# An encoder on one core: input and memory also laid out feature-major by the host, and the residual's chunks issued behind the second block of weights

## The chip, the cores and the metric

One core of one Trainium2 chip runs the whole kernel in one launch. The metric is the device time of an execution in microseconds; the time before is 2916.61 us, the median of three runs (2915.35 to 2917.63). The engines are named as the profile names them: PE (TensorE, the matrix engine) with its weight loads PEld, DVE (VectorE), ACT (ScalarE), POOL (GpSimd) and SP (SyncE), which issues most of the transfers.

## What is computed

Two layers of an encoder trunk over 256 tokens of 2048 features, in float32, with 256 memory tokens. Cut to what matters here:

```python
for layer in range(2):
    h = rms_norm(x, norm_mix_g[layer])
    if layer == 0:                       # conv module and differential attention, one input projection
        z = h @ ab_w_in                  # 2048 -> val 1024, gate 1024, q 1024, k 1024, v 1024
        a_out = silu(layer_norm(depthwise_conv(val * sigmoid(gate))))
        b_out = diff_attention(q, k, v)  # 8 heads, needs lambda from four small vectors
        x = x + concat(a_out, b_out) @ ab_w_out
    else:
        x = x + mixer_s5(h, ...)         # diagonal state space, forward and backward
    xn, memn = rms_norm(x, norm_xa_g[layer]), rms_norm(mem, norm_mem_g[layer])
    x = x + cross_attention(xn, memn)    # 4 heads; k = memn @ xa_wk, v = memn @ xa_wv
    x = x + conv_ffn(rms_norm(x, norm_ffn_g[layer]))
return rms_norm(x, final_g)
```

`rms_norm(x, g)` is `x * rsqrt(mean(x*x) + eps) * g`, the mean over the features of a token.

## The kernel before

**Products.** Every float32 operand of a large product is split in two: an upper part `hi` (rounded to the matrix engine's float32r type) and a lower part `lo` (the rest), and a product is the sum of hi x hi, hi x lo and lo x hi. The weights come from memory in tiles ("blocks") of 128 x 1024 elements, 512 KB. `wtile` (L204) issues the transfer of one on SP (L208; the very first one on ACT's queue), rounds it to `hi` on ACT (L214) and subtracts on DVE to get `lo` (L216). Four `raw` buffers and three each of `hi` and `lo` let this run ahead of PE. `lin_ws` (L242) multiplies with the weights as the stationary operand: 16 steps of 128 features, each with two products of 512 columns (`hi` against both parts of x, L254) and two of 256 columns (`lo` against x's upper part, L255), four steps to a tile of weights. `lin_xs` (L266, products in L289) does it with x as the stationary operand.

**The feature-major operand.** A product sums over features, so x must stand with features on the partitions. `transpose_chunk` (L150) makes this from 512 features of a token-major chunk: 8 transposes on PE through `ident` into two PSUM tiles `ps_xt` (L160), and from these four upper parts on ACT, scaled by the norm's gain (L167), and four lower parts on DVE (L168); the result is one buffer `x2` of four steps. The factor rstd of the norm is applied after the product: `sumsq` (L128) takes sums of squares on ACT (L132), `norm_end` (L183) turns them into `rstd` by a chain of small operations on DVE (L112 to L122, L137 and L138) and spreads it over the partitions with four small products on PE, `rb` (L147).

**The start.** `setup` (L79) loads `ident`, the first chunk of X and the gains. `mixer0` (L351) then multiplies x with the blocks of `ab_w_in`: four pairs of val and gate. For the first val block `xt_first` (L194) brings X's other three chunks in on SP (L199), one step ahead of their use, and transposes each. Behind the first `lin_ws` stand five loads of small constants (L376), the squares of X, and `norm_end`; `rb2` is used first by the first gate. `lambda` of the differential attention comes after the gates (L397 to L401).

**The memory.** `mem_T` (L305) is called after the projections of the first layer (`mem_T(0)`) and behind the first feed-forward network for the second layer (`mem_T(1)`). For layer 0 it loads all of the memory token-major into `mm`, in slot A1 (L312), sums its squares and makes the four chunks with `transpose_chunk`; for layer 1 it loads it again in eight pieces of 256 KB, `mst` (two buffers, L320), and transposes with other gains. `mem_kv` (L333) multiplies with `xa_wv` and `xa_wk`.

**Side work.** While weights stream, pieces of other work go to DVE, ACT and POOL: parameters of the state space, the convolution. `background` (L220) plays them behind each tile of weights by credits (`RATE`, L32). In the same manner `self.loads` holds loads that wait for a tile of weights: `wtile` takes one entry from it behind each tile's transfer (`load_one`, L554), until now for the heads of the cross-attention only. The framework's scheduler then sets the order on each engine, so that instructions may come earlier or later than the code has them.

## Time and profile before

| what | value |
|---|---|
| median of three runs (lowest to highest) | 2916.61 us (2915.35 to 2917.63) |
| the profiled execution: its own time | 2915.32 us |
| the profiled execution: span of the trace | 2913.5 us |
| PE busy | 2869.7 us, 98% |
| DVE busy | 2203.7 us, 76% |
| ACT busy | 1492.0 us, 51% |
| POOL busy | 266.0 us, 9% |
| DMA | 674.16 MB, mean 231 GB/s |

The busy shares are means over the whole span, in which the stages differ; the span is that of the profiled execution, 1.8 us shorter than the execution's own time, and that lies 1.3 us below the median. PE's row is the one nearest to the span. Matmuls overlap in a pipeline, so the length of one in the trace is not what it costs: what one costs is read from how far it pushes the next start.

### The profile page before, as it was taken

The numbers are of one execution on the slowest core, as the hardware profiler recorded it, in microseconds if no ns is written. First come the engines' busy times: TensorE is split into PE (matmuls) and PEld (weight loads), VectorE is DVE, ScalarE is ACT, GpSimd is POOL, SyncE is SP. The second block draws the span as 40 slices with busy tenths as digits, with TensorE's granted clock in tenths as the row PEclk, the third lists the DMA queues.
The fourth block names the chain that finished last, engine by engine and source line by source line (L and its number), as shares of the span: only waits on it lengthen the run. The fifth ranks groups of instructions, "written<-read, shape, count | busy, mean of one in ns | idle before, by whom it ended". The sixth has DMA issues, their size and how long they took to land. (4 is left out here: it accounts for less than half of the span.)

```text
span 2913.5 us, 44430 instructions
## 1 busy us (share of the span) xinstructions
PE 2869.7 (98%) x16769; PEld 2426.1 (83%) x16769; DVE 2203.7 (76%) x3524; ACT 1492.0 (51%) x2015; POOL 266.0 (9%) x504
## 2 busy tenths in 40 slices
PE   8999999999999999999999999999999999999998
PEld 7887887788888888888887787788888888888887
DVE  8899987877899987889855895556557776467765
ACT  6545654444555543455544554545445555345543
POOL 2000022222220012020021121000000000000000
PEclk9999999999999999999999999999999999999999
DMA  7655569978897688777797887665455555655554
GB/s 233 227 192 171 191 216 306 295 238 286 295 313 242 229 276 254 267 252 240 235 316 271 291 331 275 208 197 185 159 200 184 193 185 191 194 188 191 186 194 159
DMA packets 206503, 674.16 MB, mean 231 GB/s; under 512 B 33392, under 2 KB 36208, under 8 KB 205776
## 3 DMA queue, kind: packets, MB, share of 16 engines
q1 hardware_dynamic: 177952, 593.97, 61.5%
q0 software_dynamic: 28192, 76.83, 8.0%
q8 instruction: 131, 2.15, 0.3%
q14 instruction: 84, 0.69, 0.1%
q10 hardware_dynamic: 144, 0.52, 0.0%
HBM read 620.48 MB, written 61.08 MB: 234 GB/s over the span
## 5 line engine op out<-in xcount | busy, mean ns | idle before, releaser
L216 DVE TENSOR_TENSOR lo<-raw,hi 128x1024 fp32r<-128x1024 f32 x960 | 1173.1, 1223 | 539.9 <-ACT hi L214 535.8
L214 ACT CAST hi<-raw 128x1024 fp32r<-128x1024 f32 x960 | 1008.8, 1052 | 983.1 <-PE ps_xs L289 430.7
L254 PE MATMUL ps_ws<-x,hi 128*128 128x512 f32 x4352 | 1351.4, 396 | 2.8 <-DVE x L168 1.2
L255 PEld LDWEIGHTS ps_ws<-x,lo 128*128 128x128 f32 x4352 | 793.6, 188 | 186.6 <-DVE lo L216 10.5
L255 PE MATMUL ps_ws<-x,lo 128*128 128x256 f32 x4352 | 844.7, 280 | 6.7 <-DVE lo L216 6.6
L254 PEld LDWEIGHTS ps_ws<-x,hi 128*128 128x128 f32 x4352 | 674.5, 189 | 17.3 <-ACT hi L214 2.5
L289 PE MATMUL ps_xs<-hi,hb 128*128 128x512 f32 x1328 | 357.6, 390 | 0.0
L289 PEld LDWEIGHTS ps_xs<-hi,hb 128*128 128x128 f32 x1328 | 248.9, 188 | 51.7
L289 PE MATMUL ps_xs<-lo,hb 128*128 128x512 f32 x664 | 204.9, 390 | 0.0
L289 PE MATMUL ps_xs<-hi,x 128*128 128x512 f32 x640 | 177.5, 394 | 1.5 <-ACT hi L214 1.5
L852 POOL DMA_DIRECT2D w1s<-d_pw x256 | 122.8, 488 | 602.5 <-DVE w1s L845 318.2
L289 PEld LDWEIGHTS ps_xs<-hi,x 128*128 128x128 f32 x640 | 119.1, 188 | 32.0 <-issue 6.2
L289 PEld LDWEIGHTS ps_xs<-lo,hb 128*128 128x128 f32 x664 | 124.3, 188 | 25.5
L289 PE MATMUL ps_xs<-hi,oT 128*128 128x512 f32 x512 | 141.1, 392 | 0.8 <-ACT hi L214 0.8
L289 PE MATMUL ps_xs<-hi,gT 128*128 128x512 f32 x512 | 138.2, 391 | 0.3 <-ACT hi L214 0.3
L262 ACT COPY z<-ps_ws 128x512 f32<-128x512 f32 x88 | 51.7, 587 | 145.2 <-PE ps_ws L254 145.2
L289 PEld LDWEIGHTS ps_xs<-hi,gT 128*128 128x128 f32 x512 | 95.7, 188 | 21.2 <-issue 0.8
L289 PEld LDWEIGHTS ps_xs<-hi,oT 128*128 128x128 f32 x512 | 95.3, 188 | 20.1 <-ACT hi L214 1.0
L656 ACT ACTIVATE c<-z,fdb,fdw 128x256 f32<-128x256 f32 x176 | 96.3, 595 | 30.5 <-DVE z L651 30.4
L511 DVE SCALAR_TENSOR_TENSOR av<-hpt,cdw,av 128x256 f32<-128x256 f32 x240 | 109.8, 484 | 0.5
L263 DVE TENSOR_TENSOR z<-ps_ws,z 128x512 f32<-128x512 f32 x88 | 60.7, 690 | 56.0 <-ACT z L262 55.7
L289 PE MATMUL ps_xs<-lo,x 128*128 128x512 f32 x320 | 100.9, 394 | 0.0
(286 smaller groups left out, 2619.5 us busy)
## 6 DMA issues: line engine op xcount, KB each, us to landing
raw<-ffn_w_up SPq DMA_DIRECT2D x352, 512.0 KB, 3.8
raw<-ffn_w_down SPq DMA_DIRECT2D x176, 512.0 KB, 4.3
raw<-xa_wv SPq DMA_DIRECT2D x64, 512.0 KB, 3.8
raw<-xa_wk SPq DMA_DIRECT2D x64, 512.0 KB, 4.2
raw<-xa_wq SPq DMA_DIRECT2D x64, 512.0 KB, 4.3
raw<-xa_wo SPq DMA_DIRECT2D x64, 512.0 KB, 4.2
raw<-ab_w_in SPq DMA_DIRECT2D x63, 512.0 KB, 3.9
w1s<-d_pw POOLq DMA_DIRECT2D x256, 64.0 KB, 5.8
```

The source lines that it names most:

```text
L214: nc.scalar.copy(hi, raw)
L216: ins = nc.vector.tensor_tensor(lo, raw, hi.bitcast(F32), op=ALU.subtract)
L254: both = lambda c: nc.tensor.matmul(ps[:, c], lhsT=hi[:, kk, sl[c]], rhs=x2, start=first, stop=last)
L255: low = lambda c: nc.tensor.matmul(ps[:, c, 1], lhsT=lo[:, kk, sl[c]], rhs=xh, start=False, stop=False)
L262: self.nc.scalar.copy(out, ps[:, :, 1])
L263: self.nc.vector.tensor_tensor(out, ps[:, :, 0], out, op=ALU.add)
L289: ins = mm()
L511: nc.vector.scalar_tensor_tensor(ac[:, ct, :], hp[:, ct, j : j + NTOK], cdw[:, ct, j : j + 1], ac[:, ct, :], op0=ALU.mult, op1=ALU.add)
L656: nc.scalar.activation(c[:, i], zt[:, i, 1 : NTOK + 1], AF.Identity, bias=fdb[:, ft : ft + 1], scale=w(1))
L852: nc.gpsimd.dma_start(pw[t * 16 : t * 16 + 16], self.d_pw[t, k * 4 : k * 4 + 4].partition_broadcast(16))
```

## The change

The host gives x and the memory in a second layout as well, features on the partitions: `xT` and `memT`, four chunks of 512 features each.

- `feature_chunk` takes the place of `transpose_chunk` for the first norm of x and for the memory in both layers. It has the same four operations on ACT and four on DVE, reading the loaded chunk in SBUF; there is no transpose and no PSUM tile. 96 transposes go: 32 of X, 64 of the memory.
- x comes through `xraw`, in slot B2 (used later by `qk`). X itself, the residual, is needed by then for the squares only; its four chunks, `ident` and the small constants are entries of `self.loads` and so are issued behind the tiles of the second block of weights (`w[4]`, the first gate), one entry a tile. The squares go with them, and `norm_end` is written behind that block.
- Layer 0 loads the memory twice: feature-major into `mm` (slot A1), token-major into two buffers `mst` of tag "s", for the squares. Layer 1 loads it once, feature-major, in eight pieces.
- DMAs on SP: four more for `xT`, four more for `mem` in layer 0, 512 KB each.

```diff
@@ setup
         self.X = C.tile([128, 2, D], F32, name="X")
         self.ident = C.tile([128, 128], F32, name="ident")
-        nc.sync.dma_start(self.ident, a["ident"])
-        nc.sync.dma_start(self.X[:, :, 0:512], a["x"][0])
@@ new, behind transpose_chunk
+    def feature_chunk(self, raw, n, gi):
+        nc = self.nc
+        x2 = self.S.tile([128, 4, 2, NTOK], F32R, tag=f"x2{n}", name="x2")
+        for kk in range(4):
+            g = self.gains[:, gi, n * 4 + kk : n * 4 + kk + 1]
+            r = raw[kk // 2][:, kk % 2]
+            nc.scalar.activation(x2[:, kk, 0], r, AF.Copy, scale=g)
+            nc.vector.scalar_tensor_tensor(x2[:, kk, 1], r, g, x2[:, kk, 0].bitcast(F32), op0=ALU.mult, op1=ALU.subtract)
+        return x2
@@ xt_first
         for m in range(len(self.xT), min(n, 3) + 1):
-            if m:
-                self.nc.sync.dma_start(self.X[:, :, m * 512 : m * 512 + 512], self.a["x"][m])
-            self.xT.append(self.transpose_chunk(self.xslice(m), m, 0))
+            raw = self.xraw[:, m * 4 : m * 4 + 4]
+            self.nc.sync.dma_start(raw, self.a["xT"][m])
+            self.xT.append(self.feature_chunk([raw[:, 0:2], raw[:, 2:4]], m, 0))
@@ mem_T
-            mm = self.S.tile([128, 2, D], F32, tag="A1", name="mm")
+            mm = self.S.tile([128, 16, NTOK], F32, tag="A1", name="mm")
             for n in range(4):
-                nc.sync.dma_start(mm[:, :, n * 512 : n * 512 + 512], a["mem"][n])
+                nc.sync.dma_start(mm[:, n * 4 : n * 4 + 4], a["memT"][n])
         for n in range(4):
-            m = []
-            for tb in range(2):
-                if layer == 0:
-                    m.append(mm[:, tb, n * 512 : n * 512 + 512])
-                else:
-                    t = self.M.tile([128, 512], F32, tag="c0", name="mst", bufs=2)
-                    nc.sync.dma_start(t, a["mem"][n, :, tb])
-                    m.append(t)
             if layer == 0:
-                self.sumsq(m, n)
-            self.mT.append(self.transpose_chunk(m, n, 6 + layer))
+                t = self.M.tile([128, 2, 512], F32, tag="s", name="mst", bufs=2)
+                nc.sync.dma_start(t, a["mem"][n])
+                self.sumsq([t[:, 0], t[:, 1]], n)
+                raw = [mm[:, n * 4 + i * 2 : n * 4 + i * 2 + 2] for i in range(2)]
+            else:
+                raw = [self.M.tile([128, 2, NTOK], F32, tag="c0", name="mst", bufs=2) for _ in range(2)]
+                for i in range(2):
+                    nc.sync.dma_start(raw[i], a["memT"][n, :, i * 2 : i * 2 + 2])
+            self.mT.append(self.feature_chunk(raw, n, 6 + layer))
@@ mixer0, first pair of blocks
                 self.xT = []
+                self.xraw = S.tile([128, 16, NTOK], F32, tag="B2", name="xraw")
                 self.xt_first(0)
                 pv = self.lin_ws(w[n], self.xt_first)
-                for t, v in ((cdw, a["conv_dw"]), ...):
-                    nc.sync.dma_start(t, v)
+                def residual(m):
+                    if m == 1:
+                        nc.sync.dma_start(self.ident, a["ident"])
+                    if m == 3:
+                        for t, v in ((cdw, a["conv_dw"]), ...):
+                            nc.sync.dma_start(t, v)
+                    dma = nc.sync.dma_start(self.X[:, :, m * 512 : m * 512 + 512], a["x"][m])
+                    self.sumsq(self.xslice(m), m)
+                    return dma
                 self.norm_begin()
-                for i in range(4):
-                    self.sumsq(self.xslice(i), i)
-                self.norm_end()
-                rb2 = self.rb.unsqueeze(1).broadcast_to([128, 2, NTOK])
+                for m in range(4):
+                    self.loads.append((None, partial(residual, m)))
...
             val = self.add_parts(hp[:, ct, 15 : NTOK + 15], pv)
             pg = self.lin_ws(w[4 + n], self.xt)
+            if n == 0:
+                self.norm_end()
+                rb2 = self.rb.unsqueeze(1).broadcast_to([128, 2, NTOK])
@@ load_one
         src, dst = self.loads.pop(0)
+        if src is None:
+            return dst()
@@ host
+    feat = lambda x: c(x.T.reshape(4, 4, 128, NTOK).transpose(0, 2, 1, 3))
+    o["xT"] = feat(i["x"][0])
+    o["memT"] = feat(i["mem"][0])
```

The scheduler's order on the engines, of the built programs, shows what this moves. A row is the line, the operation, output and inputs with their sizes, and how many stand in a row. In the changed kernel `wtile`'s lower part is L225 instead of L216, the products L263 and L264 instead of L254 and L255, the transfer of weights L217 instead of L208, side work L242 instead of L233, the loads of the memory L321, L325 and L331 instead of L312 and L320.

PE at the very start, before:

```order
L160 MATMUL ps_xt<-ident,X 128x128 x16
L254 MATMUL ps_ws<-x_105,hi 128x512 x2
L255 MATMUL ps_ws<-x_105,lo 128x256 x4
L254 MATMUL ps_ws<-x_105,hi 128x512 x2
L255 MATMUL ps_ws<-x_105,lo 128x256 x2
L254 MATMUL ps_ws<-x_105,hi 128x512 x2
L160 MATMUL ps_xt<-ident,X 128x128 x4
```

and with the change:

```order
L263 MATMUL ps_ws<-x_105,hi 128x512 x2
L264 MATMUL ps_ws<-x_105,lo 128x256 x4
L263 MATMUL ps_ws<-x_105,hi 128x512 x2
L264 MATMUL ps_ws<-x_105,lo 128x256 x2
L263 MATMUL ps_ws<-x_105,hi 128x512 x2
```

The first instruction of PE is now a product of the first block; sixteen transposes stood ahead of it, and sixteen more among the products of that block.

DVE around the chain that makes rstd of x (`msv`, `rsq_i`, `rsq_t`), before. `x_203` and `x_251` are lower parts of x's last chunks, `lp` and `lam` belong to lambda, `PT` and `s5dt` are side work; the `lo` in these rows is the fourth split of weights on DVE:

```order
L168 SCALAR_TENSOR_TENSOR x_203<-ps_xt,gains,x_203 128x256
L397 TENSOR_TENSOR lp<-lq 128x128
L137 TENSOR_REDUCE msv<-ss 128x2
L233 SCALAR_TENSOR_TENSOR s5dt<-s5dt,s5s 128x2
L398 TENSOR_REDUCE le<-lp 128x2
L138 TENSOR_SCALAR msv<-msv 128x2
L233 TENSOR_SCALAR PT<-PT,s5dt 128x64 x2
L216 TENSOR_TENSOR lo<-raw,hi 128x1024
```

and with the change, where the `lo` is the ninth split:

```order
L418 TENSOR_TENSOR lam<-le 128x1
L242 TENSOR_TENSOR PT<-PT 128x128
L419 TENSOR_SCALAR lam<-lam 128x1
...
L135 TENSOR_REDUCE msv<-ss 128x2
L136 TENSOR_SCALAR msv<-msv 128x2
L110 TENSOR_SCALAR rsq_i<-msv 128x2
L111 TENSOR_SCALAR rsq_i<-rsq_i 128x2
...
L120 SCALAR_TENSOR_TENSOR rsq_i<-rsq_t,rsq_i 128x2
L118 TENSOR_TENSOR rsq_t<-rsq_i 128x2
L225 TENSOR_TENSOR lo<-raw,hi 128x1024
```

The chain has moved from ahead of the fourth split of weights to ahead of the ninth, behind lambda, and its first nine steps stand in one piece.

SP at the second pass over the memory (`mem_T(1)`), before. `ffn_w_down` is the down projection of the first feed-forward network, `d_w` a transfer of the state space's side work:

```order
L320 DMA mst<-mem 128x512
L208 DMA raw<-ffn_w_down 128x1024 x3
L938 DMA d_w_90<-w2o 128x1024
L208 DMA raw<-ffn_w_down 128x1024 x5
L320 DMA mst<-mem 128x512
L208 DMA raw<-ffn_w_down 128x1024 x3
L320 DMA mst<-mem 128x512 x2
L208 DMA raw<-ffn_w_down 128x1024 x2
L979 DMA d_x<-X 128x512 x2
L320 DMA mst<-mem 128x512 x2
L208 DMA raw<-ffn_w_down 128x1024 x3
L320 DMA mst<-mem 128x512 x2
```

and with the change:

```order
L331 DMA mst<-memT 128x512
L217 DMA raw<-ffn_w_down 128x1024 x2
L331 DMA mst<-memT 128x512
L217 DMA raw<-ffn_w_down 128x1024
L958 DMA d_w_88<-w2o 128x1024
L217 DMA raw<-ffn_w_down 128x1024 x2
L331 DMA mst<-memT 128x512
L217 DMA raw<-ffn_w_down 128x1024 x2
L331 DMA mst<-memT 128x512
L217 DMA raw<-ffn_w_down 128x1024
L331 DMA mst<-memT 128x512
L217 DMA raw<-ffn_w_down 128x1024 x3
```

The eight pieces come one by one with one to three blocks of weights between them, where before they came mostly in pairs. A piece's buffer comes free when ACT and DVE have read it; before, when PE had transposed it.

## Rows read from the trace of the kernel before

**Rows 1.** The page: busy time of each engine (us, share of the span, instructions).

```profile
PE 2869.7 (98%) x16769; PEld 2426.1 (83%) x16769; DVE 2203.7 (76%) x3524; ACT 1492.0 (51%) x2015; POOL 266.0 (9%) x504
```

**Rows 2.** Busy time by stretch, of the whole core: the stretch and its length in us, busy us (and instructions) of PE, its weight loads (PEld), DVE, ACT and POOL; then the granted clock, the share of time in which the DMA engines were busy, and GB/s.

```profile
30.00:400.00 370.00, 370.00 (x1979) 313.61 (x1978) 334.74 (x743) 199.44 (x327) 23.68 (x35) 1.00 0.61 199
...
200.00:300.00 100.00, 100.00 (x460) 80.82 (x459) 95.49 (x209) 56.18 (x93) 0.00 (x0) 1.00 0.54 179
...
420.00:560.00 140.00, 129.67 (x608) 103.94 (x607) 112.70 (x164) 65.97 (x92) 38.52 (x81) 0.99 0.94 299
1400.00:1500.00 100.00, 100.00 (x542) 83.84 (x541) 68.04 (x87) 51.35 (x71) 17.67 (x27) 1.00 0.80 266
```

**Rows 3.** The memory's transposes (PSUM tile `ps_xt`): engine, operation and tile with the count, the shortest, median and longest duration in ns, the first and the last start in us, the form. Then two lines of the page, operations of 256 columns that read SBUF: count, busy us, mean ns of one, idle time before them.

```profile
L160 PE MATMUL ps_xt<-ident,mm x32: 270/272/273, 103.9 to 243.4; 128*128 128x128 f32 x32
...
L160 PE MATMUL ps_xt<-ident,mst x32: 270/272/273, 1420.2 to 1465.7; 128*128 128x128 f32 x32
...
L656 ACT ACTIVATE c<-z,fdb,fdw 128x256 f32<-128x256 f32 x176 | 96.3, 595 | 30.5 <-DVE z L651 30.4
L511 DVE SCALAR_TENSOR_TENSOR av<-hpt,cdw,av 128x256 f32<-128x256 f32 x240 | 109.8, 484 | 0.5
```

**Rows 4.** PE in order of time around eight transposes of the first pass: start and length in us, engine, line, operation, output and inputs, count (of several in a row the length is from the first start to the last end).

```profile
236.29 1.03 PE L160 MATMUL ps_xt<-ident,mm 128*128 128x128 f32 x8
237.08 0.71 PE L289 MATMUL ps_xs<-lo,x 128*128 128x512 f32 x2
237.63 1.07 PE L289 MATMUL ps_xs<-hi,x 128*128 128x512 f32 x4
238.54 0.62 PE L289 MATMUL ps_xs<-lo,x 128*128 128x512 f32 x2
```

**Rows 5.** PE in order of time at the start of the program (columns as in rows 4; in brackets the idle time before and what ended it).

```profile
6.56 1.94 PE L160 MATMUL ps_xt<-ident,X 128*128 128x128 f32 x8 [6.56 <-DMA X<-x]
...
10.38 1.20 PE L254 MATMUL ps_ws<-x,hi 128*128 128x512 f32 x2
11.38 1.04 PE L255 MATMUL ps_ws<-x,lo 128*128 128x256 f32 x4
...
35.97 0.60 PE L147 MATMUL ps_rb<-dg,ones 128*128 128x128 f32 x4
...
36.88 1.10 PE L254 MATMUL ps_ws<-x,hi 128*128 128x512 f32 x4
...
41.08 0.63 PE L254 MATMUL ps_ws<-x,hi 128*128 128x512 f32 x2
...
42.47 0.63 PE L254 MATMUL ps_ws<-x,hi 128*128 128x512 f32 x2
```

**Rows 6.** ACT at the start (columns as in rows 4): the first square of X, with what it waited for, and the first upper part of x. Then stretches of the start (columns as in rows 2).

```profile
6.45 0.63 ACT L132 ACTIVATE junk<-X 128x512 f32<-128x512 f32 x1 [0.67 <-DMA X<-x]
...
7.83 0.46 ACT L167 ACTIVATE x<-ps_xt,gains 128x256 fp32r<-128x256 f32 x1
...
6.00:8.00 2.00, 1.44 (x7) 1.47 (x8) 1.55 (x5) 1.52 (x5) 0.00 (x0) 1.00 0.95 300
...
10.50:11.00 0.50, 0.50 (x4) 0.40 (x3) 0.10 (x1) 0.50 (x3) 0.00 (x0) 1.00 1.07 426
6.00:18.00 12.00, 11.18 (x59) 9.96 (x60) 9.60 (x30) 11.00 (x29) 0.00 (x0) 1.00 1.02 377
```

**Rows 7.** DVE at the start (columns as in rows 4): the first split of weights, two lower parts of x, the fifth split and the lower part behind it, the sum of two partial accumulators, the tenth split.

```profile
5.81 1.23 DVE L216 TENSOR_TENSOR lo<-raw,hi 128x1024 fp32r<-128x1024 f32 x1 [5.81 <-ACT hi L214]
...
13.41 0.87 DVE L168 SCALAR_TENSOR_TENSOR x<-ps_xt,gains,x 128x256 fp32r<-128x256 f32 x2
...
22.63 1.22 DVE L216 TENSOR_TENSOR lo<-raw,hi 128x1024 fp32r<-128x1024 f32 x1
23.76 0.48 DVE L168 SCALAR_TENSOR_TENSOR x<-ps_xt,gains,x 128x256 fp32r<-128x256 f32 x1
...
29.50 0.69 DVE L263 TENSOR_TENSOR hpt<-ps_ws,hpt 128x512 f32<-128x512 f32 x1
...
35.40 1.23 DVE L216 TENSOR_TENSOR lo<-raw,hi 128x1024 fp32r<-128x1024 f32 x1 [0.18 <-ACT hi L214]
```

**Rows 8.** The stretch ahead of the first attention's heads (columns as in rows 2), and the scores of its eight heads on DVE (columns as in rows 3).

```profile
220.00:240.00 20.00, 20.00 (x94) 16.66 (x93) 19.70 (x38) 12.33 (x20) 0.00 (x0) 1.00 0.57 184
...
L441 DVE CUSTOM_DVE_ANT_0 s<-ps_s,nb x32: 412/419/425, 250.8 to 382.0; 128x256 f32<-128x256 f32 x32
```

**Rows 9.** The two stops of PE between 420 and 430 us (columns as in rows 5).

```profile
422.16 0.50 PE L255 MATMUL ps_ws<-x,lo 128*128 128x256 f32 x2 [1.17 <-DVE lo L216]
...
426.37 0.73 PE L254 MATMUL ps_ws<-x,hi 128*128 128x512 f32 x2 [1.13 <-DVE lo L216]
```

**Rows 10.** The second pass over the memory: SP's waits for PE at its loads from 1400 to 1480 us (us in total, times, the longest), the landing of these loads, two upper parts of it on ACT, an upper part of weights on ACT, and from the page the blocks of the down projection (count, size, median us to landing).

```profile
SPq L320 <- PE ps_xt L160: 2.5, 3, 1.3
...
DMA to landing us min/median/max: 3.6/5.1/5.6
...
1441.81 0.84 ACT L167 ACTIVATE x<-ps_xt,gains 128x256 fp32r<-128x256 f32 x2 [1.54 <-PE ps_xt L160]
...
1474.14 1.05 ACT L214 CAST hi<-raw 128x1024 fp32r<-128x1024 f32 x1 [1.67 <-PE ps_xs L289]
...
raw<-ffn_w_down SPq DMA_DIRECT2D x176, 512.0 KB, 4.3
```

More of the change, by code (lines that the diff above doesn't have):

```diff
@@ L372, in mixer0 @@
                 self.xT = []
+                self.xraw = S.tile([128, 16, NTOK], F32, tag="B2", name="xraw")
                 self.xt_first(0)
                 pv = self.lin_ws(w[n], self.xt_first)
-                for t, v in ((cdw, a["conv_dw"]), (cv, a["conv_v"]), (lq, a["diff_l"].partition_broadcast(128)), (nabs, a["nabs"]), (sub_g, a["subln_g"])):
-                    nc.sync.dma_start(t, v)
+                def residual(m):
+                    if m == 1:
+                        nc.sync.dma_start(self.ident, a["ident"])
+                    if m == 3:
+                        for t, v in ((cdw, a["conv_dw"]), (cv, a["conv_v"]), (lq, a["diff_l"].partition_broadcast(128)), (nabs, a["nabs"]), (sub_g, a["subln_g"])):
+                            nc.sync.dma_start(t, v)
+                    dma = nc.sync.dma_start(self.X[:, :, m * 512 : m * 512 + 512], a["x"][m])
+                    self.sumsq(self.xslice(m), m)
+                    return dma
                 self.norm_begin()
-                for i in range(4):
-                    self.sumsq(self.xslice(i), i)
-                self.norm_end()
-                rb2 = self.rb.unsqueeze(1).broadcast_to([128, 2, NTOK])
+                for m in range(4):
+                    self.loads.append((None, partial(residual, m)))
             else:
```

## The prediction

> **What bounds the kernel now.** I read the page first: TensorE (PE) is busy 98% of the span, VectorE (DVE) 76%, ScalarE (ACT) 51% [rows 1]. The table by stage then says where that is tight: from 30 to 400 us and from 1400 to 1500 us PE is busy in every microsecond, while DVE is at 95% from 200 to 300 us [rows 2]. So a product taken off PE there comes off the time, and an operation put on DVE may cost. Behind the start PE stops first from 420 to 560 us (10.3 us of idle time) [rows 2].
>
> **The memory's transposes.** There are 32 for each pass over the memory, in 103.7 to 243.4 us and in 1420 to 1466 us [rows 3]. Their length in the rows, 272 ns, is latency. The price is the push on the next products: with eight of them, the next pair starts 0.79 us after the first transpose and takes 0.55 instead of 0.45 us to the group behind it (four such products take 0.91), so 0.89 / 8 = 0.111 us each [rows 4]. All 64 go: 64 x 0.111 = **7.1 us**. Both stretches have PE at 100%, so this is on the path. What is late next is the weights' split: DVE has 5% free from 200 to 300 us, and the gain shortens that stretch by 2% at most [rows 2].
>
> **The start.** Before, the third block of weights begins at 37.35 us (four products from 36.88, two of each block, 0.23 apart). Two k-steps take 1.39 us (41.08 to 42.47), so a tile of weights, four, 2.78 and eight tiles 22.2; the norm's broadcast costs about 0.4 (its four products take 0.60 with their latency). The start thus costs 37.35 - 22.2 - 0.4 = 14.75 us. The first product starts at 10.38. It and the second take 0.50 us each to the next, against 0.23 later, so they run at about half pace, though the granted clock reads 1.00, the 2.4 GHz level, and PE had transposed since 6.56 [rows 5, 6].
>
> Now: the first chunk lands at about 6.45, as X's did (gains ahead of it weighs what ident weighed), then 0.46 us on ACT and 0.48 on DVE: first product at 7.4, 3.0 us earlier, and 16 transposes (1.8 us) leave the products' order. A first tile wholly at half pace would end at 13.0, after the second split of weights (11.8 by the same count as below): hidden, and up to 1.2 us if DVE were faster. But DVE becomes the limit. By its order, the work from 5.81 us to the end of the tenth split is ten splits at 1.13 (22.63 to 23.76), 16 lower parts at 0.39, two sums of 512 columns at 0.6 to 0.69, and some fifty small operations that take the rest, 12.5: 31.4 us, so it ends at 37.3 if DVE never waits. For the kernel before the same count gives 36.0, and the tenth split really ended at 36.63 [rows 5, 7]. What came in is the norm's chain, which now begins ahead of the ninth split, with lambda in front of it; they wait for the residual's last chunk, for nabs and for ACT. With 0.7 to 2.3 us of waits the tenth split ends at 38.0 to 39.6. The tenth tile begins with its low part, nine tiles (25.0 us) into the stream, so the start costs 13.0 to 14.6. The gain is 0.1 to 1.7 us; I take **0.7**, nearer the low end since three waits stand in DVE's own order.
>
> The transfers bear on this. To the landing of X's last chunk the queues move 18 blocks of 512 KB and 0.8 MB of small ones, 10.2 MB. At the 377 GB/s of 6 to 18 us that takes 27.1 us from about 2 us on; at the 300 of 6 to 8 us, 34 [rows 6]. DVE reaches the chain near 33 us, and 1.5 us of squares on ACT lie between. So it is just in time. The Trainium skill's page "DMA: Bandwidth & Descriptors", section "Specifications", puts the HBM limit of a core at about 358 GB/s; by it, an estimate, the last chunk lands 1.4 us later than I take it, the start gains nothing and the sum is 7.1 instead of 7.8. This case's trace does not agree: it has 426 GB/s in a half microsecond and 377 over twelve [rows 6].
>
> The broadcast of rstd comes four tiles later. Its readers are the gates, and the accumulators are emptied ahead of them, so PE does not wait for it.
>
> The evictions stay, 16 on ACT and 16 on DVE per pass, and read from SBUF instead of PSUM. On DVE the row from PSUM is 0.48 us and the nearest from SBUF 0.484: nothing. On ACT it is 0.46 from PSUM, and the nearest of 256 columns from SBUF is 0.595 (it has a bias as well): with the 16 of x, 0 to 0.135 x 48 = 6.5 us, on an engine that is about half busy; I take nothing, and were ACT full it would be those 6.5 [rows 1, 3, 6, 7]. The first layer's memory is loaded in both layouts, 2 MB more, half of it in the first 20 us (above), the rest in a stretch where the DMA engines are busy 61% [rows 2]: nothing. POOL, 9% busy, only shifts [rows 1].
>
> **The heads of the first attention** move up by order alone: three heads' scores now come at tiles 58 to 64 instead of 84 to 90, ahead of 220 to 240 us, where DVE is busy 19.7 of 20 us. Per head that is four rows of 0.42 us on DVE, two of 0.48 and some ten small ones [rows 8]. DVE can be three tiles of weights (8 us) ahead, having three "lo" buffers; the same burst from 250 us on stopped PE nowhere [rows 2]. In return the last heads leave, ten tiles earlier, the place where PE lost 1.17 and 1.13 us at 422 and 426 us [rows 9]. Bounds: a gain of 2.3, if these two stops (both wait for "lo", the weights' lower part on DVE) go, and a loss of 2.3, if two such stops come near 200 us. I take 0, as the work is the same.
>
> **The second pass's loads.** Seven of the eight now wait for DVE; behind them on SP stand the weights of the down projection. SP's waits for PE there were 2.5 us in three [rows 10]; I take 0 and bound it under C.
>
> **Sum.** 7.1 + 0.7 = 7.8 us off 2915.32, the profiled execution (span 2913.5 and 1.8 around it): 2907.5. The median of the runs is 1.3 above that execution: **2908.8 us**. A measurement of this kernel tells 0.2%, 5.8 us, from no change: faster means below 2910.8, slower above 2922.4.
>
> **Rivals.**
> A, *the start gives back*. X's last chunk lands at 36 us, at the 300 GB/s of 6 to 8 us [rows 6]; the squares end at 37.5, the chain takes 1.2, the ninth split ends at 39.8 and the tenth 2.6 later: 42.4 - 25.0 = 17.4, so the start costs 2.7 us more than before. 7.1 - 2.7 = 4.4: 2912.2. For it: 3 MB more (X a second time and half the memory) go through one queue by then, and lambda waits for nabs as well. Against: the mean from 6 to 18 us. The page named above speaks for it by 1.4 of the 7 us that it needs. Chance 0.25.
> B, *more than the sum*. DVE hardly waits, the first product's 3.0 us stay, and the stops at 422 and 426 us go: 7.1 + 3.0 + 2.3 = 12.4: 2904.2. Against: the count of DVE's work. Chance 0.12.
> C, *slower*: SP stuck at the second pass's loads. A load may go once the half two before it has landed (5.1 us) and been read (ACT 0.84, DVE 0.87): 6.8 us. A block of weights goes out four tiles ahead (4 x 2.78 = 11.1 us) and needs 4.3 to land, 1.05 and 1.23 for its split: 4.5 us to spare. Past that it decides: if SP waits 6.8 at each of six loads, 2.3 us of each shows on PE, 14 us in all, and 2908.8 + 14 = 2922.8. For it: only one to three blocks stand between the loads. Against: two halves are in flight, so six loads need 20 us, and 15 blocks of weights give 42 [rows 7, 10]. Chance 0.06.
> D, *the gain is lost later*. From 420 to 560 us the DMA engines are busy 94% [rows 2]; if the transfers set the pace there, what the first pass saved (3.6) returns as waits: 4.2 off, 2912.4. Against: these transfers are issued tile by tile of weights, so they come earlier too. Chance 0.09.
> That the edit does not do what it says is no rival: in the order 96 transposes are gone, 32 of them of X.
>
> **The numbers.** The forecast has 0.48; most of it (0.44) lies below 2910.8. Faster: 0.44 + 0.12 = 0.56. Same: 0.04 + 0.25 + 0.09 = 0.38. Slower: 0.06. The range takes in A, B and D and leaves out C and the ends: 2903.5 to 2914.5.
>
> **What would show it.** Right: 128 transposes of X, none of mm or mst; PE at 100% from 100 to 400 us and 1400 to 1500; first product near 7.4 us; third block of weights at 36 to 37 us; DVE without a gap above 1 us from 6 to 33 us; the work behind 250 us 4 us earlier, behind 1470 us 8. Wrong: waits of PE for "lo" of over 2 us in all between 30 and 42 us (A), waits of SP at the second pass's loads of over 4.5 us (C), longer stops from 420 to 560 us (D), or a wait of PE at a head's transposes near 190 us.

## The result: 17.8 us faster, where 7.8 were forecast

| kernel | median (lowest to highest), runs | ratio to before (95% interval) |
|---|---|---|
| before | 2915.98 us (2913.49 to 2917.63), 6 | |
| with the change | 2897.44 us (2893.67 to 2899.01), 6 | 0.9939 (0.9929 to 0.9948) |
| with the change, again (E9) | 2900.45 us (2898.38 to 2904.06), 5 | 0.9950 (0.9937 to 0.9962) |

The gain is 17.8 us (15.2 to 20.7), in the second measurement 14.6 (11.1 to 18.4): both times lie below the range of the forecast, which ended at 2903.5. The profiled execution took 2897.15 us, its span 2895.0.

Busy time of the engines after, from the page; it answers to [rows 1]:

```profile
PE 2854.1 (99%) x16673; PEld 2411.6 (83%) x16673; DVE 2203.7 (76%) x3524; ACT 1492.3 (52%) x2015; POOL 265.3 (9%) x504
```

Busy time by stretch after, columns and stretches of [rows 2]:

```profile
30.00:400.00 370.00, 367.55 (x1971) 311.07 (x1970) 343.18 (x781) 210.31 (x353) 23.84 (x35) 1.00 0.60 203
200.00:300.00 100.00, 100.00 (x462) 82.44 (x461) 98.66 (x220) 57.81 (x95) 0.00 (x0) 1.00 0.58 194
420.00:560.00 140.00, 134.86 (x650) 109.86 (x650) 114.27 (x157) 64.91 (x88) 41.97 (x88) 1.00 0.96 317
1400.00:1500.00 100.00, 100.00 (x505) 82.91 (x504) 62.41 (x75) 52.07 (x72) 21.06 (x32) 1.00 0.92 312
```

PE lost 15.6 us of busy time for 96 products less, and DVE none. PE's idle time from 420 to 560 us halved, 10.3 to 5.1 us, with the work in it standing some 10 to 16 us earlier.

PE at the start after, to be read beside [rows 5]:

```profile
7.39 1.22 PE L263 MATMUL ps_ws<-x,hi 128*128 128x512 f32 x2 [7.39 <-DVE x L177]
...
34.98 0.73 PE L263 MATMUL ps_ws<-x,hi 128*128 128x512 f32 x2 [0.57 <-ACT hi L223]
36.24 0.74 PE L264 MATMUL ps_ws<-x,lo 128*128 128x256 f32 x4 [0.53 <-DVE lo L225]
```

SP's waits after from 1385 to 1465 us, the second pass's loads in the second line; they answer to [rows 10]:

```profile
SPq L217 <- DVE lo L225: 53.4, 27, 4.7
SPq L331 <- DVE x L177: 5.0, 6, 2.4
```

**Where the time came from.** Both kernels split the same 960 tiles of weights, so the start of a tile's lower part on DVE is a common mark. Tiles are counted from 0. Marks 120 and 134 before:

```profile
366.80 1.23 DVE L216 TENSOR_TENSOR lo<-raw,hi 128x1024 fp32r<-128x1024 f32 x1 [0.68 <-ACT hi L214]
...
425.11 1.21 DVE L216 TENSOR_TENSOR lo<-raw,hi 128x1024 fp32r<-128x1024 f32 x1
```

and after:

```profile
363.04 1.23 DVE L225 TENSOR_TENSOR lo<-raw,hi 128x1024 fp32r<-128x1024 f32 x1 [0.45 <-ACT hi L223]
...
415.55 1.22 DVE L225 TENSOR_TENSOR lo<-raw,hi 128x1024 fp32r<-128x1024 f32 x1
```

Fourteen tiles of the memory's k projection take 58.3 us before and 52.5 after, to 0.03 us the same in every trace that has one order or the other. No transpose of the memory stands among them; what stands there is the end of the first attention. The table gives for each kernel how many us ahead of the first trace of before it is at a mark (120 and 134: as above; 208: end of the query projection; 456 and 500: around the second pass; 959: the last tile), and the length of the stretch from 134 to 208.

| trace | 32 | 120 | 134 | 208 | 456 | 500 | 959 | 134 to 208 | ratio of the runs |
|---|---|---|---|---|---|---|---|---|---|
| before | 0 | 0 | 0 | 0 | 0 | 0 | 0 | 245.0 |  |
| before again (E10) | -1.7 | -0.4 | -0.4 | 4.2 | 3.5 | 3.5 | -1.4 | 240.4 | one run |
| change | 1.4 | 3.8 | 9.6 | 15.9 | 15.6 | 19.2 | 18.3 | 238.7 | 0.9939 |
| change again (E9) | 1.2 | 3.5 | 9.3 | 12.3 | 11.2 | 14.9 | 12.6 | 242.0 | 0.9950 |
| E1 start only | 3.9 | 4.6 | 4.6 | 9.9 | 8.7 | 8.7 | 5.2 | 239.7 | 0.9982 |
| E2 first pass only | 0.0 | 2.3 | 8.1 | 16.3 | 14.8 | 14.8 | 11.6 | 236.8 | 0.9974 |
| E3 second pass only | -0.6 | 0.1 | 0.1 | 3.3 | 1.5 | 5.2 | 0.9 | 241.9 | 0.9996 |
| E4 "ps" left to the scores | -1.2 | 0.7 | 0.7 | 6.4 | 5.6 | 5.6 | 2.7 | 239.4 | 0.9994 |
| E5 squares later | 3.3 | 5.6 | 11.4 | 13.8 | 13.4 | 14.8 | 14.9 | 242.6 | 0.9943 |
| E6 halves apart | 1.7 | 1.1 | 6.9 | 12.4 | 12.4 | 16.1 | 15.2 | 239.5 | 0.9950 |
| E7 heads held | 0.9 | 0.8 | 0.8 | 2.6 | 1.1 | 4.8 | 5.6 | 243.2 | 0.9978 |
| E8 both passes, old start | 0.4 | 2.7 | 8.5 | 14.2 | 13.1 | 16.7 | 16.2 | 239.3 | 0.9944 |
| E11 change, less side work early | 1.7 | 4.0 | 9.8 | 29.2 | 15.8 | 16.2 | 14.3 | 225.6 | 0.9941 |
| E12 E11 and E5 | 3.2 | 5.5 | 11.4 | 30.9 | 20.1 | 15.1 | 15.0 | 225.5 | 0.9938 |
| E13 before, new rates | 0.2 | -0.2 | -0.2 | 16.0 | 5.0 | 4.1 | 3.1 | 228.9 | 0.9985 |
| E14 change, new rates | 1.6 | 3.9 | 9.7 | 26.1 | 21.6 | 25.0 | 23.5 | 228.7 | 0.9916 |
| E15 E14 and E5 | 3.8 | 6.1 | 11.9 | 28.9 | 21.9 | 25.3 | 25.3 | 228.0 | 0.9907 |

At marks 120 and 134 executions of one kernel agree within 0.4 us (at mark 32 the two of before are 1.7 us apart). Behind mark 134 the stretch to 208 varies by 3 to 5 us from one execution to the next, and behind mark 500 they part again: the second trace of before loses 4.9 us there against the first. A lead at mark 208 or at the end is thus known to some 5 us by one pair of traces.

### The profile page after: what moved, and what is told of

It reads as the page before. It is cut to its first block, busy times and chain, and to the rows that moved or that the text cites. A ratio compares the mean times of both kernels' runs of the same rounds, so it can differ in the third digit from the quotient of the medians.

```text
span 2895.0 us, 44267 instructions
## 1 busy us (share of the span) xinstructions
PE 2854.1 (99%) x16673; PEld 2411.6 (83%) x16673; DVE 2203.7 (76%) x3524; ACT 1492.3 (52%) x2015; POOL 265.3 (9%) x504
## 5 line engine op out<-in xcount | busy, mean ns | idle before, releaser
L225 DVE TENSOR_TENSOR lo<-raw,hi 128x1024 fp32r<-128x1024 f32 x960 | 1173.1, 1223 | 534.6 <-ACT hi L223 530.9
L263 PE MATMUL ps_ws<-x,hi 128*128 128x512 f32 x4352 | 1350.7, 396 | 8.0 <-DVE x L177 7.4
L264 PEld LDWEIGHTS ps_ws<-x,lo 128*128 128x128 f32 x4352 | 793.3, 188 | 191.4 <-DVE lo L225 14.8
L264 PE MATMUL ps_ws<-x,lo 128*128 128x256 f32 x4352 | 846.2, 280 | 8.1 <-DVE lo L225 7.7
L263 PEld LDWEIGHTS ps_ws<-x,hi 128*128 128x128 f32 x4352 | 674.3, 189 | 21.9 <-DVE x L177 7.4
L298 PEld LDWEIGHTS ps_xs<-hi,oT 128*128 128x128 f32 x512 | 95.3, 188 | 20.1 <-ACT hi L223 1.0
```

What stands on the lines that cost most here:

```text
L225: ins = nc.vector.tensor_tensor(lo, raw, hi.bitcast(F32), op=ALU.subtract)
L263: both = lambda c: nc.tensor.matmul(ps[:, c], lhsT=hi[:, kk, sl[c]], rhs=x2, start=first, stop=last)
L264: low = lambda c: nc.tensor.matmul(ps[:, c, 1], lhsT=lo[:, kk, sl[c]], rhs=xh, start=False, stop=False)
L298: ins = mm()
```

## The experiments

The edits are cut to the lines that matter.

**Parts of the change.** E1 keeps `mem_T` and its layouts as before; E2 and E3 start from before and change `mem_T` for one layer:

```diff
# E1: the changed kernel, in mem_T
-            self.mT.append(self.feature_chunk(raw, n, 6 + layer))
+            self.mT.append(self.transpose_chunk(m, n, 6 + layer))
# E2, E3: the kernel before; E2 if layer == 0, E3 if layer == 1
+                self.mT.append(self.feature_chunk(raw, n, 6 + layer))
```

> The start alone: x feature-major and the residual behind the second block of weights; the memory is transposed on PE as before, in both passes. Theory H (the extra gain hangs on the first pass over the memory: its transposes take PSUM buffers of the tag "ps" that the first attention's scores need, so without them the heads start 26 tiles of weights earlier): only the start's own gain, 1.0 to 1.5 us, 2914.5 to 2915; the heads' scores stay from about 248 to 369 us, three heads of the eight take 2.1 us for their scores and not 1.06, and the stops of PE near 421, 425 and 503 us (1.2, 1.1 and 2.2 us) stay. Rival S (the stretch from 420 to 640 us runs better after any earlier arrival, whatever its cause): 1.2 + some 7 = 8 us faster, 2908, with shorter stops near 503 us and no fall of the granted clock there.

Measured: 2909.01 us, ratio 0.9982 (0.9974 to 0.9991), 5 us. The start gains 4.6 us to mark 134, more than four times what it does in the whole change, and more than the 1.0 to 1.5 that H gave it. The heads' place and the two stops are those of before, as H said; the low clock near 514 us is there too, and the 8 us of S did not come.

> The first pass over the memory alone is feature-major (loaded in both layouts); start and second pass as before. Theory H: 3.4 us for 32 transposes, 3.0 us for three heads whose scores are paired again, 1.7 to 2.3 us for the stops near 421 and 425 us, and what follows in the out projection and the query projection (5.7 and 1.5 us): 13 to 15 us faster, 2901 to 2903. Rival T (the transposes of this pass are the whole of it): 3.4 us, 2912.5. Rival S: 3.4 + 7 = 10.4, 2905.5, the scores' pairs bring nothing.

Measured: 2904.84 us, ratio 0.9974 (0.9963 to 0.9986). 52.5 us from mark 120 to 134, as in the change; at mark 134 it is 8.1 us ahead, at mark 500 14.8 (11.3 against E10). T alone would be 3.4, and the interval of the runs, 4.1 to 10.8 us, leaves it out; it leaves out H's 13 to 15 as well. S's 10.4 lies inside, but S gave nothing to the scores' pairs, and the scores take 8.7 us of PE here as in the change, before 11.7. The 7.6 us of the runs are what the transposes (3.7) and the place of the heads (3.9, worked out below) come to.

> The second pass over the memory alone is feature-major; everything up to it as before. Theory H and rivals S and T agree: 32 transposes at 0.111 = 3.6 us, of which 0.9 may be given back at the start of the state space stage near 1550 us: 2.7 to 3.6 us faster, 2912.4 to 2913.3. A loss here, or a wait of SP at its loads of over 4.5 us, would show that the waits of the loads count.

Measured: 2913.04 us, ratio 0.9996 (0.9987 to 1.0005), unclear by time alone. The second pass itself gives 3.7 us between the marks 456 and 500, as in the change; the 4.3 us that this trace loses behind mark 500 are no more than E10 loses there.

**Why the heads move.** PSUM, where PE writes its results, has two buffers of tag "ps" and two of tag "pt" for these small tiles. The transposes take them in turn from both tags, the scores of a head take "ps" alone. In the kernel before, the first sixteen transposes of the memory fill all four at 104 to 122 us, and the first of their results is read at 226 us:

```profile
226.11 0.83 ACT L167 ACTIVATE x<-ps_xt,gains 128x256 fp32r<-128x256 f32 x2
```

E4 leaves the transposes and gives them the other PSUM tag; E7 takes the changed kernel and holds the buffers without a transpose:

```diff
# E4, the kernel before; tag goes on to self.pst("ps_xt", tag)
-            self.mT.append(self.transpose_chunk(m, n, 6 + layer))
+            self.mT.append(self.transpose_chunk(m, n, 6 + layer, None if layer else "pt"))
# E7, feature_chunk of the changed kernel; held for layer 0's memory
+            if held:
+                if kk % 2 == 0:
+                    ps = self.pst("ps_hold")
+                    nc.tensor.matmul(ps[:, :2], lhsT=self.ident, rhs=self.gains[:, gi, n * 4 + kk : n * 4 + kk + 2], start=True, stop=True)
+                g = ps[:, kk % 2 : kk % 2 + 1]
```

> The kernel before with one edit: the 32 transposes of the first pass over the memory stay, but take PSUM buffers of the tag "pt" alone, so that the scores' tag "ps" is free. No transpose and no byte less. Theory H: the heads' scores move to about 170 us and the gain that is not the transposes' comes all the same, 7 to 11 us: 2905 to 2909; of the three heads with doubled score time at most one is left. Rival T: no change, 2915 to 2917. Rival S: no change or a pair's 2 to 3 us, 2913 to 2916.

Measured: 2912.62 us, ratio 0.9994 (0.9985 to 1.0003). Two heads' scores came early on DVE (175 and 187 us); the third's waited until 273 us and the last stayed at 381. 58.3 us from mark 120 to 134, no gain there. By the numbers set before the run, T's "no change" fits and H's 7 to 11 us did not come. Most heads stayed late, so the edit did not make the case that H speaks of: in the code a head takes "pt" too, behind its scores. That this is what held them is argued, not shown; E7 decides between H and T.

> The changed kernel, without any transpose of the memory, but each half chunk of the first pass holds a PSUM buffer until it is read, as the transposes did: a product of two columns copies the gains into it, and DVE takes its factor from there. Eight products of two columns, well under 1 us. Theory H (the buffers held the heads back): the heads' scores stand at 250 to 370 us again and the time is 6 to 10 us longer than the changed kernel's, 2903 to 2907. Rival T (the transposes' own time on PE): under 1 us longer, 2896 to 2898.

Measured: 2908.84 us, ratio 0.9978 (0.9968 to 0.9989), 11 us slower than the change beside 0.9939, 8 beside 0.9950. The holding products and the scores in E7 (columns of [rows 3]):

```profile
L180 PE MATMUL ps_hold<-gains,ident x16: 166/251/252, 89.0 to 238.1; 128*128 128x2 f32 x16
```

```profile
L464 DVE CUSTOM_DVE_ANT_0 s<-ps_s,nb x32: 415/420/426, 242.9 to 381.1; 128x256 f32<-128x256 f32 x32
```

and the scores in the changed kernel:

```profile
L459 DVE CUSTOM_DVE_ANT_0 s<-ps_s,nb x32: 411/419/425, 173.2 to 362.2; 128x256 f32<-128x256 f32 x32
```

Marks 120 and 134 of E7:

```profile
365.96 1.23 DVE L230 TENSOR_TENSOR lo<-raw,hi 128x1024 fp32r<-128x1024 f32 x1 [0.68 <-ACT hi L228]
...
424.27 1.22 DVE L230 TENSOR_TENSOR lo<-raw,hi 128x1024 fp32r<-128x1024 f32 x1
```

58.3 us again, without one transpose of the memory, and the heads are late again: T falls, and it was the hold on PSUM that set the place of the heads. At mark 134 E7 is 8.7 us behind the change, and on PE 8.1 at the end of the k projection. Not all of this is the place of the heads: the holding products take 1.45 us from their starts to the next ones ("well under 1 us" was expected) and the products beside them 1.2 more. The scores take 4.2 us more than in the change and the stops near 421 and 425 us 1.0, so the heads' place costs 5.2 us in E7. In E7 four heads of eight lose their pair (next experiment), in the kernel before three, so there it costs less, 3.9 (below).

**The scores' halves.** E6 changes the order of four products:

```diff
-            for qb in range(2):
-                for c in range(2):
+            for c in range(2):
+                for qb in range(2):
```

(each kept behind the one before.)

> The changed kernel with the scores' four products of a head in the order (first half of the rows, both query blocks; then the second half), where the changed kernel has the two halves side by side. Theory H's term for pairs (two products on the two halves of the rows run at the same time, 0.53 us for both as for one): one of the four still stands beside one of the other half, so a head takes three times 0.53 and not two: 0.53 x 8 = 4.2 us slower than the changed kernel, 2900 to 2901; up to 8.5 if none pairs. Rival (products of 64 rows cost their columns, in any order): no change, 2896 to 2897.

Measured: 2899.27 us, ratio 0.9950 (0.9937 to 0.9963), against 0.9939 and 0.9950 of the change: not told apart by time. In the trace the scores take 11.04 us of PE (starts to next starts), in the change 8.71, before 11.68, in E7 12.93: 2.3 us more, half of the 4.2 expected, and E6 is 2.7 us behind the change at mark 134. A product has two records here, a head eight. Six of E6's heads have all eight side by side and take 1.07 us, as in the change, in spite of the new order; the other two are parted by products of weights and take 4.6 together instead of 2.1. One whole head and parts of these two:

```profile
170.19 1.14 PE L457 MATMUL ps_s<-qk 64*128 64x256 f32 x8
...
194.41 1.13 PE L457 MATMUL ps_s<-qk 64*128 64x256 f32 x4
...
198.46 1.13 PE L457 MATMUL ps_s<-qk 64*128 64x256 f32 x4
```

So the term is real, but the order within a head, which I had priced, is not what costs: other products between the halves are. The kernel before has the same in three heads, here its last one:

```profile
367.32 1.13 PE L437 MATMUL ps_s<-qk 64*128 64x256 f32 x4
...
368.92 1.13 PE L437 MATMUL ps_s<-qk 64*128 64x256 f32 x4
```

and a head in the changed kernel:

```profile
346.42 1.13 PE L455 MATMUL ps_s<-qk 64*128 64x256 f32 x8
```

Eight records in 1.13 us where four took as long: with the halves of the rows side by side two products run at once.

**Adding up.**

```diff
# E5: the changed kernel; mem_T(0) without loads of mem and squares, in mixer0:
+            if n == 1:
+                self.norm_begin()
+                for m in range(4):
+                    self.loads.append((None, partial(self.mem_squares, m)))
# E8: the kernel before with the changed kernel's mem_T, both layers
```

> The changed kernel with one edit: the token-major memory, needed for its squares alone, is loaded behind the tiles of the block two gates later, as the residual's chunks are behind the first, and not in the first 6 us. Theory M (in the changed kernel the start gives back 3 us, because 1 MB of memory goes ahead of the residual and its eight squares on ACT stand between the weights' upper parts; without them E1's start gained 4.6 us where the changed kernel's gained 1.4): 3 us faster than the changed kernel, 20 to 21 faster than before, 2893 to 2894; no stop of PE between 20 and 40 us over 0.5 us. Rival (DVE's own order sets the start, 37 us, whatever else moves): the changed kernel's time, 2896 to 2897.

Measured: 2898.28 us, ratio 0.9943 (0.9929 to 0.9957). The start is quicker, as M said (no stop of PE over 0.5 us from 20 to 40 us), but the 3 us do not reach the end: 1.9 us ahead of the change at marks 120 to 134, behind it at 208. The seventh split of weights starts 3.2 us earlier in E1 than in the change; in the change it is

```profile
27.21 1.22 DVE L225 TENSOR_TENSOR lo<-raw,hi 128x1024 fp32r<-128x1024 f32 x1
```

and in E1 24.06 us. Two blocks of memory, 1.05 MB, at 398 GB/s (6 to 18 us after) are 2.6 us, an estimate. E1 and E5 take the early blocks and their squares on ACT out together, so what each of the two costs is not shown.

> The start as before, both passes over the memory feature-major. If the parts add: E2's 7.6 to 9.2 and 2.7 to 3.6 for the second pass, 10 to 13 us faster than before, 2901 to 2904, and the whole change (17.8) is this and 5 to 7 us more from the start. Theory M: less, as the start gains only 1.4 us net in the changed kernel where the memory comes early: 16 us faster, 2898.

Measured: 2898.08 us, ratio 0.9944 (0.9931 to 0.9957). As M said: the new start adds 0.8 to 1.1 us to this at mark 134, and nothing that the runs can show. The parts do not quite add up in the runs: E2's 7.6 us and E3's 1.2 are 8.8, E8 has 16.3 (12.5 to 20.1). Their intervals hardly explain this, and it stays open.

**The stretch from 134 to 208.**

```diff
# E11 (the change)
-"out": 0.8, "wq": .7, "wo": .8, "up": .75, "down": 0.96
+"out": 0.4, "wq": .35, "wo": .9, "up": .8, "down": 1.0
# E13 (before), E14 (the change), E15 (E5's kernel)
+"out": 0.4, "wq": .35, "wo": .8, "up": .75, "down": 1.36
```

> The changed kernel once more, beside the next three on one chip. Up to the 134th tile of weights the traces so far repeat within 0.1 us for one kernel; from there to the 190th (425 to 604 us before) seven kernels took 171.7 to 179.2 us with no order in it but the heads' place. If that stretch varies from execution to execution, this trace takes 172 to 177 us there where the first of the changed kernel took 172.9, and the time is 16 to 18 us below before, 2896 to 2898. If it is the kernel's own, the stretch is 172.9 again within 0.5 us.

> The kernel before once more, one look. If the stretch of the 134th to the 190th tile varies from execution to execution: 174 to 178 us where the first trace has 179.2, and the stop of PE near 503 us (2.2 us there) 1.2 to 3.2. If it is the kernel's own: 179.2 within 0.5. The three heads with doubled scores and the stops near 421 and 425 us (1.17 and 1.13 us) are the order's own by both and stay to 0.05 us.

Measured: E9 176.7 us from mark 134 to 190 where the first trace has 172.9; E10 2916.68 us, with 175.3 where the first has 179.2. The stretch varies with the execution, and the first two traces were far apart by chance: 6.3 of their 18.5 us come from it, and the two later ones are 1.5 us apart the other way. (What E9's text says of traces that agree to 0.1 us was too narrow: the table has up to 0.4.) E10 has the stops near 421 us again and the scores' 11.67 us.

> The changed kernel with half the rate of side work in the out projection and the query projection (0.8 and 0.7 credits a tile become 0.4 and 0.35), and a little more later (wo 0.8 to 0.9, up 0.75 to 0.8, down 0.96 to 1.0). Theory D2 (in this stretch the transfers of the side work, 1 MB in and out per step, set the pace beside the weights): the stops of PE from 434 to 640 us, some 10 us, fall to under 4, the 134th to the 190th tile takes 166 us, and the time is up to 6 us below the changed kernel's, unless the up projection, where DVE is over 90% busy, takes it back. Rival (the weights alone fill the queues): stops and time as in the changed kernel, 2896 to 2898.

Measured: 2898.37 us, ratio 0.9941 (0.9928 to 0.9953), no better than the change. The stretch from 134 to 208, and the up projection (marks 240 to 416), in the change:

```profile
415.55:654.25 238.70, 229.87 (x1232) 193.00 (x1231) 191.04 (x273) 113.93 (x154) 61.28 (x128) 1.00 0.89 292
753.91:1260.03 506.12, 506.12 (x3392) 433.99 (x3390) 452.52 (x682) 255.72 (x319) 58.27 (x99) 1.00 0.78 261
```

and in E11:

```profile
415.33:640.95 225.62, 224.46 (x1224) 192.76 (x1223) 168.39 (x232) 114.57 (x154) 34.33 (x72) 1.00 0.79 262
743.45:1260.03 516.58, 508.56 (x3269) 434.11 (x3268) 461.92 (x696) 254.90 (x318) 80.59 (x146) 0.99 0.81 272
```

D2 holds: with less side work the DMA engines are busy 79% instead of 89%, PE idles 1.2 us instead of 8.8, 13 us are gained. DVE has 23 us less to do as well, but the waits show the transfers: the rounding of the weights on ACT waited 62 us for its blocks to land in the change,

```profile
ACT hi L223 <- DMA raw<-xa_wq: 31.4, 13, 4.8
ACT hi L223 <- DMA raw<-ab_w_out: 30.6, 18, 5.2
```

and 22 in E11:

```profile
ACT hi L223 <- DMA raw<-xa_wq: 11.1, 6, 3.1
ACT hi L223 <- DMA raw<-ab_w_out: 10.8, 7, 3.7
```

The up projection then takes 10.5 us more, 8.0 of them idle PE; the rest goes behind it. E12, E11's rates with E5's squares, was expected at about 2890 and came to 2898.98 us, the same: its lead is given up in the up projection and behind it too.

> The kernel before with the side work of the out and query projections at half rate (0.4 and 0.35 credits a tile) and made up in the down projection alone (0.96 to 1.36), where DVE is 68% busy; up and wo keep their rates. E11 showed that this takes the stops out of the 134th to the 190th tile (164.2 us, stops 1.1 us after the 134th). By the same the kernel before should gain 8 to 14 us there and keep it, as the up projection is not loaded more: 2901 to 2907. Beside E14 it gives the change's worth with that stretch calm: if the change is worth only its countable terms (start 1.0, transposes 3.7 and 3.7, scores' pairs 3.0, stops near 421 us 1.3), E14 is 12.7 us below this kernel; if the stretch belongs to the change's gain by itself, 16 us or more.

> The changed kernel with E13's rates. Theory D2: the 13 us that E11 had gained at the 208th tile and lost in the up projection stay: 8 to 13 us below the changed kernel, 2885 to 2890. Rival (DVE's work is conserved and the down projection or the state space's start takes it back): 2896 to 2899. Against E13: 12.7 us if the countable terms are the whole, 16 or more if not.

Measured: E13 2910.32 us, ratio 0.9985 (0.9976 to 0.9995); E14 2890.46 us, ratio 0.9916 (0.9902 to 0.9929). E13:

```profile
425.25:654.10 228.85, 225.10 (x1218) 192.55 (x1218) 169.98 (x246) 115.54 (x161) 34.33 (x72) 0.99 0.78 256
754.93:1270.00 515.07, 510.30 (x3338) 434.94 (x3337) 471.63 (x717) 255.09 (x319) 84.41 (x154) 1.00 0.85 277
```

and E14:

```profile
415.40:644.06 228.66, 225.96 (x1224) 192.43 (x1223) 168.37 (x232) 114.67 (x154) 34.33 (x72) 1.00 0.80 260
744.88:1253.38 508.50, 507.48 (x3338) 433.99 (x3337) 470.63 (x716) 255.25 (x319) 84.37 (x154) 1.00 0.84 280
```

With the stretch calm the change is worth 9.9 us at mark 134 and 10.0 at 208: the stretch itself adds nothing. E13 was expected to keep its gain and did not: 16.0 us ahead at mark 208, 5.0 at 456, since the up projection took 515.1 us where the kernel before has 506.1. E14 kept more and came within half a microsecond of its forecast. The two differ by 20 us in the runs, which is the "16 or more" of the expectation and not its 12.7. By the marks 10.0 us of it stand at 208, 6.6 arise in the up projection, where PE idles 4.8 us in E13 and 1.0 in E14, and 4.3 around the second pass. One trace of each does not show whether those 6.6 belong to the change or to the execution.

> E14 with E5's later squares of the memory. With the stretch calm, E5's 1.9 us at the 134th tile should come through: 1.9 us below E14 (2883 to 2888), or the same within 0.5 if something later takes it back, as in E5 and E12.

Measured: 2889.65 us, ratio 0.9907 (0.9894 to 0.9921), the lowest of all, by the ratios 9 to 13 us below the change. Against E14 the trace is 2.2 us ahead at mark 134, 0.3 at 500 and 1.8 at the end; the runs (0.8) do not tell them apart.

## Why the prediction was wrong, by its steps

The time from each product's start to the next on PE, summed by tile up to the end of the memory's k projection (its last product starts at 455.7 us before, at 446.8 after), gives the terms.

- *64 transposes, 7.1 us.* Right. The first pass took 2.92 us and slowed the products behind it by 0.82; the second gives 3.7: 7.4.
- *Evictions, nothing.* Right: four upper parts from SBUF take 1.71 us, 0.43 each, where one from PSUM had 0.46 [rows 6]:

```profile
6.01 1.71 ACT L176 ACTIVATE x<-xraw,gains 128x256 fp32r<-128x256 f32 x4 [0.33 <-DMA xraw<-xT]
```

- *The start, 0.7.* Right in size, by luck: 0.9 (5.25 for X's transposes, less 3.5 that the first products take longer and 0.8 of the first start). First product at 7.39 (forecast 7.4), third block at 34.98 (36 to 37), tenth split at 38.6 (38.0 to 39.6). Wrong in its reason: DVE's count was no limit, as E1 ends the tenth split at 35.0 with the same operations, though in another order. What held it was "2 MB more ... nothing": with 1 MB of memory ahead of the residual, and the memory's squares, the tenth split ends 3.3 to 3.6 us later than in E5 and E1.
- *The heads, 0, as the work is the same.* **This is the step that failed.** The move is no accident of the order: "ps_xt" took half of its PSUM buffers from the tag that the scores need, and held them from 104 until its readers came at 226 us. (By the code those wait for the last reader of x, whose buffers the memory's parts take.) Without the hold the scores go in pairs (3.0 us: 11.68 to 8.71) and the stops at 421 and 425 us, 2.3 [rows 9], become one of 1.36 at 396 us: 0.9. That is 3.9 us instead of 0. Work that is the same can take another time, and I had bounded it by the two stops alone. My fear, a wait near 200 us, did not come: PE is busy in every microsecond from 200 to 300.
- *Second pass's loads, 0.* Right, though SP waited 5.0 us there, over the 4.5 that I had set as C's sign: PE was busy in all of 1400 to 1500 us, so the sign was too near.
- *Rivals.* A's stops are 1.1 us (34 to 36 us), not over 2. D was wrong in kind: the stretch from 134 to 208 does not give back what came before, nor does it belong to this change. Rival B named the right stops and not their cause.

The countable terms are 0.9 + 3.7 + 3.0 + 0.9 + 3.7 = 12.2 us, 4.4 more than the forecast's 7.8, and 3.9 of these are the heads'. The runs have 14.6 to 17.8, so the failed step explains 3.9 of the 6.8 to 10.0 us that the forecast lacked. From 134 to 208 six traces with late heads (before, E10, E3, E4, E1, E7) take 241.6 us in the mean and six with early ones (change, E9, E2, E8, E5, E6) 239.8: 1.8 more, less than one kernel's own variation. Even with it 0.6 to 3.8 us stay open. In the first pair of traces the clock had a part, of a size that no run here gives: PE was granted 0.91 of full speed from 500 to 520 us before, behind a stop of 2.23 us, some of it at the 1.2 GHz level:

```profile
500.00:520.00 20.00, 16.14 (x65) 11.97 (x64) 13.84 (x19) 11.07 (x18) 3.83 (x8) 0.91 0.86 280
```

and 1.00 after from 480 to 500, where the same products stand:

```profile
480.00:500.00 20.00, 18.55 (x85) 14.78 (x84) 15.15 (x20) 10.21 (x17) 7.18 (x16) 1.00 0.91 288
```

E9 has low clock there too, at 498 us.

## What to carry to other kernels

Ask of every operation that an edit removes which buffers it held and who waited for them; a move that the order shows has a cause, and what it costs is found by holding the buffer without the work, as E7 does, with the cost of the holding counted out. Mark two traces by a count that both share: the stage where they part shows at once, and which part of a difference is one execution's. A gain ahead of a stretch that is paced by transfers is judged in the runs, several of each, and moving side work out of it helps only where another stage has room (13 us gained and lost in E11, kept in part in E14).

## What the runs showed of the hardware

Two products on 64 rows each, on the two halves of the rows, start 7 to 14 ns apart and run at once: 1.13 us for eight records as for four. The Trainium skill's page "TensorE: Matmul & The Clock Gate", section "Why this matters for your kernels", says that products with few rows run concurrently when they lie in distinct row groups, and gives it for four of 32 rows; this case shows it for two of 64. What I had not expected is that the place of the halves in the instruction order decides it: where the scheduler puts other products between them the pair is lost, in three heads of eight before, in none after, and in two in E6.
